# Splitting the second layer's weights and rows ahead of time, and a bank's products in one run

## The chip, the cores and the metric

One NeuronCore of a Trainium2 chip runs the whole program. The metric is the device time of one execution in microseconds (us). TensorE does the matrix products, VectorE (DVE) and ScalarE (ACT) read its results out of PSUM and prepare its operands, GpSimd (POOL) helps on SBUF data alone, and nearly all transfers between DRAM and SBUF are issued in order by SyncE's queue (SP).

## The reference

A row block x of 2048 tokens by 1024 goes through one retention layer and one layer of windowed attention. Cut to what matters:

```python
# layer 1, retention: 4 heads, chunks of 128 rows, a running state S per head
proj = rmsnorm(x, a_norm_g) @ a_w_in          # q, k, v (4x512), gate (4x512)
o = rms(retention(q, k, v)) * silu(gate)
x = x + o @ a_w_out
# layer 2, attention over the row's own and the previous block of 128 rows
k, v = split(rmsnorm(x, kv_norm_g) @ w_kv);  k = rmsnorm(k, k_norm_g)     # 2 kv heads of 64
q, gate = split(rmsnorm(x, b_norm_g) @ b_w_in);  q = rmsnorm(q, b_q_norm_g)  # 16 heads of 64
p = softmax(q @ k.T / 8 + bias, masked, with a sink per head)
x = x + ((p @ v) * silu(gate)) @ b_w_out
# rms(x) = x * rsqrt(mean(x * x) + 1e-6)
```

## The kernel before

Every product of float32 operands is made of three float32r products of a high and a low part: `hi*hi`, `hi*lo`, `lo*hi`. The high part is a ScalarE copy to float32r, the low part is what the subtraction leaves. All four banks of a projection (`pbank`, tags a and b with two buffers each) are taken by every projection, so the next one can write bank 0 only when bank 0 of the one before has been read out.

The rows are taken in 4 groups of 512 (`T`). **Phase a** is the retention: 16 units, one for each group and head. A unit is `main` (the projections `project_qk` and then `plain_vg` or, from unit 4 on, `strassen`), `ret` (the recurrence over 4 chunks) and `out_a` (two halves of `out_proj`, which adds into the residual rows `x1`). `drive` interleaves the `main` of one unit with the `ret` of the unit before. Small staging work (`stage_sums`, `row_stats`, `stage_rows`) is a generator in the list `behind`, one step of which is emitted at each `step()`, 18 of them in a unit with `strassen`. When a group's last head is out, its rows go to DRAM (`xmid`) and their sums of squares to `sqs`.

**Phase b** is the attention: 8 units, one for each group and key/value head. `work` yields the projections in order (`keys` once a group, `queries`, `gates`, `out_b`, and `out_last` for the last unit), and `plan` says how many of these steps go into each of 66 slots, between which one chunk of attention (`scores`, `scale`, `turn`, `values`, `gated`) is emitted. The agenda (`at`) adds small work some steps later. The steps and the plan fix the program order; a scheduler of the framework orders each engine's queue from it.

What the change touches in phase b: `wload` loads a piece of weights of 128 x 1024 and splits it (ACT copy on L127, subtraction on POOL on L132, or on DVE on L134 when the weights are first scaled by the norm's gain on L124 and kept in DRAM). `prep` does this for group 0's rows at the end of phase a, after multiplying them by the row norm (L195); `rows` does it for groups 1 to 3 with POOL's multiplication on L964, ACT's copy on L968 and DVE's subtraction on L969. Those rows' tiles have one buffer, so a group's rows go in when the gates of the group before have been computed.

Of the kernel before, what the change touches and what calls it, by code (L numbers as in the profile page):

```python
# [12 lines left out]
F32 = mybir.dt.float32  # L13
# [6 lines left out]
P = 128  # L20
D = 1024
# [15 lines left out]
PIECE = 512  # L37
# [21 lines left out]
def tile_yoco(ctx, tc, x, x_t, w_qk, w_vg, wo_a, w_kv, w_b, wo_b, ag, kvg, bg, kng, qng,  # L59
# [15 lines left out]


# [34 lines left out]
    scaled = {}  # L111

    def wload(src, cols, name, kscale=None, key=None):

        kn = 1024 // cols
        if key in scaled:
            src, kscale = scaled[key], None
# [4 lines left out]
        if kscale is not None:  # L122
            for k in range(kn):
                nc.vector.tensor_scalar_mul(raw[:, k, :], raw[:, k, :], kscale[:, k : k + 1])  # L124
            scaled[key] = dram.tile([P, kn, cols], F32, name=f"ws_{name}")
            nc.sync.dma_start(scaled[key], raw)
        nc.scalar.copy(hi, raw)  # L127
        if psum["phase"] == "b" and kscale is None:

            for k in range(0, kn, PIECE // cols):  # L130
                t = (slice(None), slice(k, k + PIECE // cols))
# [5 lines left out]
    def proj(src, nk, xhi, xlo, feat, evac, name, kscale=None, key=None, cols=512, before=None):  # L137
        kn = 1024 // cols
        bk = [pbank("ab"[m // 2], f"pp_{name}_{m}") for m in range(4)]
        for kp in range(nk // kn):  # L140
            if before is not None:
                before(kp)
            hi, lo = wload(src[kp], cols, f"{name}_{kp}",
                           None if kscale is None else kscale[:, kp * kn : (kp + 1) * kn],
                           (key, kp))
            for kk in range(kn):
                k = kp * kn + kk
                st, sp = k == 0, k == nk - 1
                kx = xhi[0].shape[1]
                xh, xl = xhi[k // kx][:, k % kx, :], xlo[k // kx][:, k % kx, :]  # L150
                for m in range(4):
                    sl = slice(m * P, (m + 1) * P)
                    o = bk[m][:, :cols]
# [8 lines left out]
            yield  # L162
        for m in range(4):
            evac(m, bk[m])
# [6 lines left out]
    def stats(g, tiles, tag):  # L171
# [6 lines left out]
        ss = small.tile([P, MT], F32, tag="ssx", bufs=2, name=f"ssb_{g}")  # L178
        nc.vector.tensor_copy(ss, ps[:, :MT])
        r = rsqrt_mean(ss, D, MT, f"b_{g}")  # L180
# [4 lines left out]
        rb = small.tile([P, T], F32, tag="rb", bufs=1, name=f"rb_{g}")  # L185
        nc.vector.tensor_copy(rb, rp)
        return rb

    def prep(g, rb):

        xhi, xlo = xt_tiles(f"b{g}")
        for kp in range(KT // 2):
            raw = wp.tile([P, 2, T], F32, tag="raw", bufs=RAW, name=f"xraw_b{g}_{kp}")
            nc.sync.dma_start(raw, xmid[g][kp])
            nc.vector.tensor_tensor(raw, raw, rb.unsqueeze(1).to_broadcast([P, 2, T]), op=ALU.mult)  # L195
            hi, lo = xhi[kp], xlo[kp]
            nc.scalar.copy(hi, raw)
            nc.vector.tensor_tensor(lo, raw, hi.bitcast(F32), op=ALU.subtract)
            yield
        return xhi, xlo  # L200

    def out_proj(src, ohi, olo, evac, name):
        for half in range(2):
            yield from proj(src[half], 4, ohi, olo, True,
                            lambda m, ps, half=half: evac(half * 4 + m, ps), f"{name}_{half}")
# [22 lines left out]
    first = {}  # L228


    def phase_a(pa):
# [110 lines left out]

        def strassen(n, src, xt, evac, after):
# [13 lines left out]
            for p in range(7):  # L357
# [3 lines left out]
                for i, w in enumerate(src(p)):  # L361
                    hi, lo = wload(w, 512, f"{n}_{p}{i}")
                    for kk in range(2):
                        k = i * 2 + kk
                        if p in (0, 1, 6):
                            k0 = k + KT // 2 * (p > 0)
                            xh, xl = (t[k0 // 2][:, k0 % 2, H * (p == 6) :] for t in xt)
                        else:
                            xh, xl = (t[:, k, :] for t in st["sum", SX[p - 2]])
                        start, stop = k == 0 and p in (0, 1, 3), k == KT // 2 - 1  # L370
                        for f in range(2):
                            sl = slice(f * P, (f + 1) * P)
# [301 lines left out]
        def prep_b0():  # L674
            rb = stats(0, [short(f"st_{i}") for i in range(2)], "rr")
            first["xt"] = yield from prep(0, rb)

        def out_a(u):
            g, h = units[u]
            ohi, olo, x1 = st.pop(("o", u))  # L680
            acc = []

            def evac(f, ps):
# [9 lines left out]
                if f == 0:  # L693
                    acc.append(stp(f"acc_{g}"))
                    nc.gpsimd.tensor_copy(acc[0], sq)
                else:
                    nc.gpsimd.tensor_tensor(acc[0], acc[0], sq, op=ALU.add)
                if f == KT - 1:
                    nc.sync.dma_start(sqs[g], acc[0])
# [14 lines left out]
        bias = bias_rows()  # L714
        for u in range(nu - 1):
# [521 lines left out]
```

## Time and profile before

| What | Value |
|---|---|
| Median of 3 runs (lowest to highest) | 2511.96 us (2510.32 to 2513.04) |
| The profiled execution: its own time, its span | 2509.29 us, 2507.5 us |
| TensorE products busy, mean granted clock | 97% of the span, 0.986 |
| VectorE, ScalarE, GpSimd busy | 67%, 45%, 20% |
| DMA queue 1 | 393 MB, 47.3% of 16 engines |

The span is the time from the first to the last instruction; the execution takes some 2 us more. A busy share says how much of a stretch an engine had an instruction in flight; the granted clock is the share of TensorE's 2.4 GHz that it was given, whose lower level is 1.2 GHz. Phase a takes the first 1652 us and phase b the rest.

### The profile page before, as it was taken

The numbers are of one execution on the slowest core, as the hardware profiler recorded it, in microseconds if no ns is written. First come the engines' busy times: TensorE is split into PE (matmuls) and PEld (weight loads), VectorE is DVE, ScalarE is ACT, GpSimd is POOL, SyncE is SP. The second block draws the span as 40 slices with busy tenths as digits, with TensorE's granted clock in tenths as the row PEclk, the third lists the DMA queues.
The fourth block names the chain that finished last, engine by engine and source line by source line (L and its number), as shares of the span: only waits on it lengthen the run. The fifth ranks groups of instructions, "written<-read, shape, count | busy, mean of one in ns | idle before, by whom it ended". The sixth has DMA issues, their size and how long they took to land.

```text
span 2507.5 us, 31994 instructions
## 1 busy us (share of the span) xinstructions
PE 2435.8 (97%) x11576; PEld 1976.3 (79%) x11576; DVE 1670.0 (67%) x2856; ACT 1118.1 (45%) x2060; POOL 495.8 (20%) x487
## 2 busy tenths in 40 slices
PE   8999999999999999999999999989899999989998
PEld 6888777888887888888888888778687777768776
DVE  5546675776867657678666576666766766676675
ACT  4333233544435445445354354435544545445452
POOL 0000000020000020000011000032444645455350
PEclk9999999999999999999999999989899999999999
DMA  8434883586636454465354343365243242342422
GB/s 291 138 111 136 261 274 118 171 288 226 233 113 199 136 180 151 151 219 182 121 193 164 101 147 113 114 241 185 76 143 128 91 148 68 135 149 87 141 94 86
DMA packets 141178, 395.09 MB, mean 158 GB/s; under 512 B 16427, under 2 KB 29020, under 8 KB 141020
## 3 DMA queue, kind: packets, MB, share of 16 engines
q1 hardware_dynamic: 141020, 393.05, 47.3%
q8 instruction: 91, 1.49, 0.2%
q14 instruction: 67, 0.55, 0.1%
HBM read 321.66 MB, written 74.47 MB: 158 GB/s over the span
## 4 chain that ended last, share of the span: by engine, by line
PE 75%; DVE 7%; DMA 4%; issue 1%; ACT 1%; POOL 0%; SPq 0%; ACTq 0%; DVEq 0%; POOLq 0%
PE pp_ao L157 4%; PE pp_ao L155 4%; PE pp_ao L156 4%; PE o_t L1052 2%; PE s_t L1003 2%; PE pp_bo L784 2%; PE pp_bo L785 2%; PE pp_bo L783 2%; PE pT_t L1034 1%; PE ot_r L649 1%; PE o_r L621 1%; PE o_r L623 1%; PE o_r L622 1%; PE dl_r L613 1%; DVE P_t L1006 1%
## 5 line engine op out<-in xcount | busy, mean ns | idle before, releaser
L107 POOL TENSOR_SCALAR r_o_r<-sso_r,ep 128x1 f32<-128x1 f32 x48 | 27.7, 578 | 910.3 <-ACT jo_r L643 910.3
L155 PE MATMUL pp_ao<-ohi_r,whi_ao 128*128 128x512 f32 x512 | 199.3, 393 | 7.5 <-DVE x_r L685 2.6
L156 PE MATMUL pp_ao<-olo_r,whi_ao 128*128 128x512 f32 x512 | 200.9, 392 | 0.0
L157 PE MATMUL pp_ao<-ohi_r,wlo_ao 128*128 128x512 f32 x512 | 196.6, 393 | 0.1
L1006 DVE CUSTOM_DVE_ANT_0 P_t<-s_t,bias,nsnk 128x256 f32<-128x256 f32 (+1 forms) x256 | 112.6, 470 | 70.1 <-PE s_t L1003 49.9
L127 ACT CAST whi_ao<-raw_ao 128x1024 fp32r<-128x1024 f32 x64 | 67.2, 1050 | 152.8 <-issue 47.3
L1016 ACT ACTIVATE P_t<-P_t,nm_t 128x128 f32<-128x128 f32 x256 | 100.5, 395 | 77.0 <-DVE P_t L1013 66.6
L134 DVE TENSOR_TENSOR wlo_ao<-raw_ao,whi_ao 128x1024 fp32r<-128x1024 f32 x64 | 78.1, 1223 | 83.2 <-ACT whi_ao L127 83.2
L1003 PEld LDWEIGHTS s_t<-kst,qst_b 128*128 128x128 f32 x512 | 78.8, 194 | 56.2 <-DVE nm_t L1006 32.1
L709 ACT CAST Shi_r<-S 128x512 fp32r<-128x512 f32 x120 | 69.9, 617 | 117.4 <-PE o_r L623 88.2
L1003 PE MATMUL s_t<-kst,qst_b 128*128 128x256 f32 (+1 forms) x512 | 96.5, 301 | 26.4 <-DVE nm_t L1006 26.1
L155 PEld LDWEIGHTS pp_ao<-ohi_r,whi_ao 128*128 128x128 f32 x512 | 96.7, 189 | 29.4 <-DVE x_r L685 3.4
L157 PEld LDWEIGHTS pp_ao<-ohi_r,wlo_ao 128*128 128x128 f32 x512 | 96.9, 190 | 21.8 <-DVE wlo_ao L134 1.4
L156 PEld LDWEIGHTS pp_ao<-olo_r,whi_ao 128*128 128x128 f32 x512 | 96.8, 189 | 20.2 <-issue 0.2
L710 DVE TENSOR_TENSOR Slo_r<-S,Shi_r 128x512 fp32r<-128x512 f32 x120 | 85.4, 737 | 40.0 <-ACT Shi_r L709 39.8
L636 DVE SCALAR_TENSOR_TENSOR S<-S,dl_r 128x512 f32<-128x512 f32 x112 | 74.7, 682 | 41.5 <-PE dl_r L615 41.3
L132 POOL TENSOR_TENSOR wlo_bo<-raw_bo,whi_bo 128x512 fp32r<-128x512 f32 x56 | 76.2, 1382 | 114.7 <-ACT whi_bo L127 75.8
L685 DVE TENSOR_TENSOR x_r<-x_r,pp_ao 128x512 f32<-128x512 f32 x128 | 83.8, 683 | 12.5 <-PE pp_ao L157 12.4
L784 PE MATMUL pp_bo<-olo_t,whi_bo 128*128 128x512 f32 x224 | 90.6, 404 | 0.0
L785 PE MATMUL pp_bo<-ohi_t,wlo_bo 128*128 128x512 f32 x224 | 89.1, 403 | 0.0
L783 PE MATMUL pp_bo<-ohi_t,whi_bo 128*128 128x512 f32 x224 | 85.5, 404 | 0.0
L107 POOL TENSOR_SCALAR r_o_r<-sso_r,es_a 128x1 f32<-128x1 f32 x16 | 8.1, 506 | 359.9 <-ACT jo_r L643 359.9
(1084 smaller groups left out, 7509.7 us busy)
## 6 DMA issues: line engine op xcount, KB each, us to landing
raw_ao<-in_wo_a SPq DMA_DIRECT2D x64, 512.0 KB, 3.6
b<-in_w_vg SPq DMA_DIRECT2D x64, 256.0 KB, 4.8
res<-xmid SPq DMA_DIRECT2D x56, 256.0 KB, 4.1
raw_bo<-in_wo_b SPq DMA_DIRECT2D x28, 512.0 KB, 3.5
x_r<-in_x_t SPq DMA_DIRECT2D x16, 512.0 KB, 6.0
xin<-in_x SPq DMA_DIRECT2D x16, 512.0 KB, 3.6
xmid<-x_r SPq DMA_DIRECT2D x16, 512.0 KB, 4.2
xraw_b<-xmid SPq DMA_DIRECT2D x16, 512.0 KB, 3.7
```

The lines of the kernel that those rows point to most:

```text
L134: nc.vector.tensor_tensor(lo, raw, hi.bitcast(F32), op=ALU.subtract)
L155: nc.tensor.matmul(o, hi[:, kk, sl], xh, start=st, stop=False)
L156: nc.tensor.matmul(o, hi[:, kk, sl], xl, start=False, stop=False)
L157: nc.tensor.matmul(o, lo[:, kk, sl], xh, start=False, stop=sp)
L685: nc.vector.tensor_tensor(t, t, ps, op=ALU.add)
L710: nc.vector.tensor_tensor(lo, src[:, d, :], hi.bitcast(F32), op=ALU.subtract)
L783: nc.tensor.matmul(o, hi[:, kk, sl], xh, start=s, stop=False)
L784: nc.tensor.matmul(o, hi[:, kk, sl], xl, start=False, stop=False)
L785: nc.tensor.matmul(o, lo[:, kk, sl], xh, start=False, stop=e)
L1003: nc.tensor.matmul(o, q[:, h, :], kst[:, kv * 2 + hl, kb + b0 : kb + 2, :], start=hl == 0, stop=hl == 1)
L1006: nc.vector.tensor_tensor_reduce(out=pt[:, j, :w], in0=o, in1=bias[:, kv * GQ + h, b0 * P :], scale=-1.0, scalar=nsnk[:, kv * GQ + h : kv ...
L1016: nc.scalar.activation(pt[:, i, :P], pt[:, i, :P], AF.Exp, scale=-1.0, bias=nm[:, i : i + 1], accum_out=den[:, i : i + 1])
```

## The change

In phase b no weights and no rows are split any more, but for the last group's rows. `stage_b` does it in phase a: in units 7, 8, 9, 11, 12 and 13 it loads nine pieces each of 128 x 512 of phase b's weights, multiplies them by the gain, makes the two parts on ACT and DVE and writes them to DRAM (`wb`). `out_a` splits the rows of groups 0 to 2 when they are complete (`split_row`, to `xb`). Phase b loads both parts straight into the operands' tiles. The rows are no longer multiplied by their norm: keys and queries are normalised anyway, with an epsilon that is scaled with the row (`eps`), values are multiplied by the row's factor as they leave PSUM, and gates by a row of factors (`rb`), one more DVE operation for each bank. In `proj`, `strassen` and `proj_b` (not in `project_qk`) the loop over banks goes outside that over a piece's blocks of 128, so that 6 (keys: 12) products go to one bank one after the other where it was 3. `out_proj` loads the first piece of its second half ahead of reading out the first. The plan gives the last unit but one fewer steps and the last one more.

```diff
-    def wload(src, cols, name, kscale=None, key=None):
+    def wload(src, cols, name):
...
-        if psum["phase"] == "b" and kscale is None:
-            for k in range(0, kn, PIECE // cols):
-                nc.gpsimd.tensor_tensor(lo[t], raw[t], hi[t].bitcast(F32), op=ALU.subtract)
-        else:
-            nc.vector.tensor_tensor(lo, raw, hi.bitcast(F32), op=ALU.subtract)
+        nc.vector.tensor_tensor(lo, raw, hi.bitcast(F32), op=ALU.subtract)
...
-            for kk in range(kn):
...
-                for m in range(4):
+            for m in range(4):
...
+                for kk in range(kn):
...
+        if then is not None:
+            then()
         for m in range(4):
             evac(m, bk[m])
...
+    def load_xb(g):
+        first["xt"] = xt = xt_tiles(f"b{g}")
+        for kp in range(KT // 2):
+            if g == NG - 1:
+                raw = wp.tile([P, 2, T], F32, tag="raw", bufs=RAW, name=f"xraw_{kp}")
+                nc.sync.dma_start(raw, xmid[g][kp])
+                yield
+                nc.scalar.copy(xt[0][kp], raw)
+                nc.vector.tensor_tensor(xt[1][kp], raw, xt[0][kp].bitcast(F32), op=ALU.subtract)
+                yield
+                continue
+            for i, t in enumerate(xt):
+                nc.sync.dma_start(t[kp].bitcast(F32), xb[g][kp][:, i])
+            yield
...
+        def stage_b(pieces):
+            nxt = None
+            for n, (src, dst, scale) in enumerate(pieces + [(None,) * 3]):
+                cur = nxt
+                if src is not None:
+                    t = p1.tile(list(src.shape), F32, tag="st", bufs=6, name=f"wraw_{n}")
+                    nc.sync.dma_start(t, src)
+                    nxt = t, dst, scale
+                if cur is not None:
+                    t, d, sc = cur
+                    hi, lo = (p1.tile(list(t.shape), F32R, tag="st", bufs=6, name=f"w{hl}_{n}") for hl in ("hi", "lo"))
+                    for k in range(t.shape[1]):
...
+                            nc.scalar.mul(hi[:, k, :], t[:, k, :], sc[:, k : k + 1])
+                            nc.vector.scalar_tensor_tensor(lo[:, k, :], t[:, k, :], sc[:, k : k + 1],
+                                                           hi[:, k, :].bitcast(F32), op0=ALU.mult, op1=ALU.subtract)
+                    for i, v in enumerate((hi, lo)):
+                        nc.sync.dma_start(d[:, i], v.bitcast(F32))
+                yield
...
+            def split_row(f):
+                t = x1[f // 2][:, f % 2, :]
+                hi, lo = (p1.tile([P, T], F32R, tag="st", bufs=6, name=f"xm{hl}_{g}_{f}") for hl in ("hi", "lo"))
+                nc.scalar.copy(hi, t)
+                nc.vector.tensor_tensor(lo, t, hi.bitcast(F32), op=ALU.subtract)
+                for i, v in enumerate((hi, lo)):
+                    nc.sync.dma_start(xb[g][f // 2][:, i, f % 2, :], v.bitcast(F32))
...
-                    acc.append(stp(f"acc_{g}"))
+                    acc.append(wp.tile([P, T], F32, tag="raw", bufs=RAW, name=f"acc_{g}"))
...
+            if u + 1 in (7, 8, 9, 11, 12, 13):
+                behind.append(stage_b(todo[:9]))
+                del todo[:9]
...
-        pre = prep_b0()
-        drive(tc, itertools.chain(out_a(nu - 2), itertools.islice(pre, 2)), ret(nu - 1), 1.5, 0)
-        for _ in itertools.chain(out_a(nu - 1), pre):
+        scales(0, [short(f"stb_{i}") for i in range(2)], "rr", small.tile([P, T], F32, tag="rb", bufs=1, name="rb_0"))
+        rows = load_xb(0)
+        drive(tc, itertools.chain(rows, out_a(nu - 2)), ret(nu - 1), 2, 0)
+        for _ in out_a(nu - 1):
             pass
...
+        def parts_of(key, kp, name):
+            d = wb[key][kp]
+            t = [wp.tile([P] + list(d.shape[2:]), F32R, tag=f"w{hl}", bufs=3, name=f"w{hl}_{name}_{kp}") for hl in ("hi", "lo")]
+            for i in range(2):
+                nc.sync.dma_start(t[i].bitcast(F32), d[:, i])
+            return t
...
-                nc.scalar.activation(t, ps, AF.Tanh, scale=0.5)
-                nc.vector.scalar_tensor_tensor(t, t, 1.0, ps, op0=ALU.add, op1=ALU.mult)
+                nc.vector.tensor_tensor(t, ps, scaled[g][2], op=ALU.mult)
+                th = p1.tile([P, T], F32, tag="th", bufs=2, name=f"th_{n}_{m}")
+                nc.scalar.activation(th, t, AF.Tanh, scale=0.5)
+                nc.vector.scalar_tensor_tensor(t, th, 1.0, t, op0=ALU.add, op1=ALU.mult)
...
-        for u in range(1, nu - 1):
+        for u in range(1, nu - 2):
             plan += [4, 4] + ([4, 4, 4] if units[u + 1][1] == 0 else [3, 3, 2]) + [3, 3, 2]
-        plan += [2, 2, 2, 1, 1, 3, 3, 2, 0]
+        plan += [3, 3, 3, 3, 3, 3, 3, 1] + [1, 2, 2, 2, 2, 1, 3, 3, 2]
```

## Rows read from the trace of the kernel before

**Rows 1.** The page: the span, TensorE's busy time, and the granted clock in 40 equal slices (9 is 0.9 or more).
```profile
span 2507.5 us, 31994 instructions
PE 2435.8 (97%) x11576; PEld 1976.3 (79%) x11576; DVE 1670.0 (67%) x2856; ACT 1118.1 (45%) x2060; POOL 495.8 (20%) x487
PEclk9999999999999999999999999989899999999999
```
**Rows 2.** Busy time by stretch (us from the span's start): the stretch's length, then busy us and count of PE, PEld, DVE, ACT and POOL, the granted clock, the DMA engines' busy share and GB/s.
```profile
280.00:390.00 110.00, 101.48 (x453) 81.94 (x452) 76.19 (x102) 35.81 (x48) 3.77 (x6) 0.98 0.77 254
390.00:700.00 310.00, 310.00 (x1424) 256.33 (x1423) 223.95 (x300) 139.55 (x200) 32.07 (x34) 1.00 0.62 208
...
1600.00:1680.00 80.00, 69.94 (x342) 58.59 (x341) 57.30 (x94) 28.60 (x52) 22.00 (x24) 0.91 0.47 158
1680.00:1800.00 120.00, 112.95 (x549) 88.04 (x547) 89.46 (x205) 63.36 (x145) 41.34 (x35) 0.97 0.50 174
1800.00:1990.00 190.00, 188.20 (x968) 147.80 (x968) 121.16 (x321) 93.19 (x248) 87.71 (x77) 0.98 0.33 110
1990.00:2020.00 30.00, 22.20 (x101) 16.33 (x100) 26.47 (x52) 16.99 (x45) 17.00 (x11) 0.83 0.38 123
2020.00:2200.00 180.00, 178.78 (x931) 141.21 (x930) 114.77 (x294) 86.15 (x219) 88.17 (x76) 1.00 0.34 114
2200.00:2230.00 30.00, 22.80 (x97) 16.43 (x96) 24.70 (x49) 16.11 (x44) 15.98 (x10) 0.83 0.38 123
...
2405.00:2508.00 103.00, 89.50 (x502) 68.78 (x500) 63.88 (x177) 39.49 (x121) 20.18 (x15) 0.95 0.29 98
```
**Rows 3.** What TensorE waited for from 1600 to 1670 us: who waited for whom, us in total, times, longest.
```profile
PE pp_b0k L787 <- ACT whi_b0k L127: 4.1, 1, 4.1
PE ot_r L649 <- DVE gate_a L646: 2.7, 1, 2.7
PE pp_b0k L787 <- DVE x_r L685: 0.7, 1, 0.7
```
**Rows 4.** The same from 1990 to 2030 us.
```profile
PE s_t L1003 <- DVE nm_t L1006: 7.4, 2, 4.0
```
**Rows 5.** VectorE from 1985 to 2020 us in order of time: start, us, instruction.
```profile
1998.59 1.78 DVE L874 TENSOR_TENSOR qs_b<-qn_b,qs_b 128x512 fp32r<-128x512 f32 x1
2000.29 2.29 DVE L969 TENSOR_TENSOR xlo_b<-xraw_b,xhi_b 128x1024 fp32r<-128x1024 f32 x1
...
2007.44 0.68 DVE L874 TENSOR_TENSOR qs_b<-qn_b,qs_b 128x512 fp32r<-128x512 f32 x1
...
2014.22 1.22 DVE L969 TENSOR_TENSOR xlo_b<-xraw_b,xhi_b 128x1024 fp32r<-128x1024 f32 x1
```
**Rows 6.** GpSimd in the same stretch.
```profile
1999.78 3.93 POOL L964 TENSOR_TENSOR xraw_b<-xraw_b,rb 128x512 f32<-128x512 f32 x2
2007.55 3.90 POOL L964 TENSOR_TENSOR xraw_b<-xraw_b,rb 128x512 f32<-128x512 f32 x2 [3.85 <-DMA xraw_b<-xmid]
```
**Rows 7.** TensorE in the middle of a projection: L155 to L157 are the three products of one block into one bank, and the next L155 goes to the next bank.
```profile
606.37 0.39 PE L156 MATMUL pp_ao<-olo_r,whi_ao 128*128 128x512 f32 x1
606.59 0.39 PE L157 MATMUL pp_ao<-ohi_r,wlo_ao 128*128 128x512 f32 x1
606.82 0.39 PE L155 MATMUL pp_ao<-ohi_r,whi_ao 128*128 128x512 f32 x1
```
**Rows 8.** Groups of instructions of the page: busy us and mean ns of one, idle before, and what ended it.
```profile
L127 ACT CAST whi_ao<-raw_ao 128x1024 fp32r<-128x1024 f32 x64 | 67.2, 1050 | 152.8 <-issue 47.3
L134 DVE TENSOR_TENSOR wlo_ao<-raw_ao,whi_ao 128x1024 fp32r<-128x1024 f32 x64 | 78.1, 1223 | 83.2 <-ACT whi_ao L127 83.2
L709 ACT CAST Shi_r<-S 128x512 fp32r<-128x512 f32 x120 | 69.9, 617 | 117.4 <-PE o_r L623 88.2
L710 DVE TENSOR_TENSOR Slo_r<-S,Shi_r 128x512 fp32r<-128x512 f32 x120 | 85.4, 737 | 40.0 <-ACT Shi_r L709 39.8
L132 POOL TENSOR_TENSOR wlo_bo<-raw_bo,whi_bo 128x512 fp32r<-128x512 f32 x56 | 76.2, 1382 | 114.7 <-ACT whi_bo L127 75.8
L685 DVE TENSOR_TENSOR x_r<-x_r,pp_ao 128x512 f32<-128x512 f32 x128 | 83.8, 683 | 12.5 <-PE pp_ao L157 12.4
```
**Rows 9.** DMA issues of the page: tensor, count, size, median us from issue to landing.
```profile
b<-in_w_vg SPq DMA_DIRECT2D x64, 256.0 KB, 4.8
...
raw_bo<-in_wo_b SPq DMA_DIRECT2D x28, 512.0 KB, 3.5
```
**Rows 10.** Busy time by stretch as in rows 2, in units 10 and 11 (unit 11 begins at 1117 us).
```profile
1070.00:1090.00 20.00, 20.00 (x102) 16.88 (x101) 18.93 (x29) 12.96 (x20) 1.58 (x2) 1.00 1.00 339
...
1110.00:1130.00 20.00, 20.00 (x91) 16.46 (x91) 8.53 (x11) 6.32 (x9) 1.34 (x2) 1.00 0.19 66
1130.00:1150.00 20.00, 20.00 (x93) 16.44 (x93) 12.20 (x19) 5.96 (x9) 0.82 (x2) 1.00 0.26 78
```
**Rows 11.** Waits of the whole span: VectorE for the staged weights of `stage_sums`.
```profile
DVE b L335 <- DMA b<-in_w_vg: 30.5, 11, 5.5
```
**Rows 12.** What TensorE waited for from 2400 to 2510 us.
```profile
PE pT_t L1034 <- DVE P_t L1028: 4.3, 1, 4.3
PE s_t L1003 <- DVE nm_t L1006: 3.7, 4, 1.1
```

More of the change, by code (lines that the diff above doesn't have):

```diff
@@ L74, in tile_yoco @@
     sqs = [dram.tile([P, T], F32, name=f"sqs{i}") for i in range(NG)]
+    parts = lambda shape, name: dram.tile([P, 2] + shape, F32, name=name)
+    xb = [[parts([2, T], f"xb{i}_{kp}") for kp in range(KT // 2)] for i in range(NG - 1)]
+    wb = {"k": [parts([4, 256], f"wk{kp}") for kp in range(2)]}
+    for kv in range(KVH):
+        wb["q", kv], wb["g", kv] = ([parts([2, T], f"w{n}{kv}_{kp}") for kp in range(4)] for n in "qg")
+        for half in range(2):
+            wb["o", kv, half] = [parts([2, T], f"wo{kv}{half}_{kp}") for kp in range(2)]
     neghalf = const.tile([P, GQ], F32, name="neghalf")
@@ L184, in stats, with ahead @@
         nc.tensor.matmul(rp, ones, dg, start=True, stop=True)
-        rb = small.tile([P, T], F32, tag="rb", bufs=1, name=f"rb_{g}")
         nc.vector.tensor_copy(rb, rp)
[L187 to L200, printed above, removed]
-    def out_proj(src, ohi, olo, evac, name):
-        for half in range(2):
-            yield from proj(src[half], 4, ohi, olo, True,
-                            lambda m, ps, half=half: evac(half * 4 + m, ps), f"{name}_{half}")
+        scaled[g] = r, eps, rb
+    def out_proj(src, ohi, olo, evac, name):
+        pre = []
+        def ahead():
+            pre.extend(wload(src[1][0], 512, f"{name}_1_0"))
+        yield from proj(src[0], 4, ohi, olo, True, evac, f"{name}_0", then=ahead)
+        yield from proj(src[1], 4, ohi, olo, True, lambda m, ps: evac(4 + m, ps), f"{name}_1", first=pre)
     bdr = dram.tile([QH, P, 384], F32, name="bdr")
@@ L362, in strassen @@
                     hi, lo = wload(w, 512, f"{n}_{p}{i}")
[L363 to L372, printed above, removed]
+                    for f in range(2):
+                        sl = slice(f * P, (f + 1) * P)
+                        for kk in range(2):
+                            k = i * 2 + kk
+                            if p in (0, 1, 6):
+                                k0 = k + KT // 2 * (p > 0)
+                                xh, xl = (t[k0 // 2][:, k0 % 2, H * (p == 6) :] for t in xt)
+                            else:
+                                xh, xl = (t[:, k, :] for t in st["sum", SX[p - 2]])
+                            start, stop = k == 0 and p in (0, 1, 3), k == KT // 2 - 1
                             kw = dict(skip_group_check=True)
@@ L697, in evac @@
                     nc.gpsimd.tensor_tensor(acc[0], acc[0], sq, op=ALU.add)
+                if f % 4 == 3 and g < NG - 1:
+                    for i in range(f - 3, f + 1):
+                        split_row(i)
                 if f == KT - 1:
-                    nc.sync.dma_start(sqs[g], acc[0])
+                    if g == NG - 1:
+                        first["acc"] = acc[0]
+                    else:
+                        nc.sync.dma_start(sqs[g], acc[0])
             yield from out_proj(wo_a[h], ohi, olo, evac, f"ao{u}")
@@ L759, in phase_b @@
         nchunk = nu * MT * 2
-        st = {"xt": first["xt"], "step": 0}
+        st = {"step": 0}
         agenda = {}
@@ L789, in proj_b @@
                             nc.tensor.matmul(o, xl[:, sl], hi[:, kk, :], start=False, stop=e)
-                    if not e and (kk + 1) * cols % 512 == 0:
+                    if m == 1 or m == 3 and kp < nk // kn - 1:
                         yield
@@ L800, in keys @@
             n = f"b{g}k"
-            yield from proj_b(w_kv, KT, st["xt"], False, n, kscale=kvgs, key="kv", cols=256)
+            yield from proj_b("k", KT, first["xt"], False, n, cols=256)
+            r_x, eps = scaled[g][:2]
             if g and not kb:
@@ L1102, in work @@
                 if u + 2 < nu and units[u][1] == 0:
-                    at(12, scales, units[u + 2][0])
-                yield from out_b(u - 1)
-                if u + 1 < nu:
+                    at(12, row_scales, units[u + 2][0])
+                if u < nu - 1:
+                    yield from out_b(u - 1)
                     if units[u + 1][1] == 0:
```

147 lines of the change are left out of this document (70 added, 77 removed).

## The prediction

> **What bounds the kernel now.** I read the page first: TensorE has products in flight for 2435.8 of 2507.5 us and the granted clock is full in all but two of 40 slices [rows 1]. So at most some 72 us of idle time and a little lost clock can be won unless the products themselves get shorter. They don't: their number is unchanged, and in the middle of a projection one starts every 0.22 or 0.23 us, both within a bank (L156 to L157) and where the next bank begins (L157 to L155) [rows 7]. I take 0.227 us.
>
> Next came the busy time by stretch, to see where the missing time lies [rows 2]. The loss of a stretch is its idle time plus the clock that was not granted, (1 - granted) x length. From 390 to 700 us it is 0, with VectorE busy for 224 of 310 us; from 2020 to 2200 us it is 1.2. The loss is in clumps:
>
> - 1600 to 1680, where the retention ends: 10.1 + 0.09 x 80 = 17.3 us.
> - 1680 to 1800, first attention units: 7.1 + 3.6 = 10.7.
> - 1800 to 1990: 1.8 + 3.8 = 5.6.
> - 1990 to 2020, rows of group 2 coming in: 7.8 + 0.17 x 30 = 12.9.
> - 2200 to 2230, the same for group 3: 7.2 + 5.1 = 12.3.
> - 2405 to 2508, the tail: 13.5 + 5.2 = 18.7.
>
> Together 77.5 us, and outside phase b another 10.7 at 280 to 390 (8.5 + 2.2). Then the waits and the order of time in the clumps. At the first, keys' products wait 4.1 us for the ACT copy of the first weights, behind the rows' preparation [rows 3]. At the third, scores wait 7.4 us for VectorE in two waits [rows 4]; VectorE is subtracting row parts there, 2.29 us for one while GpSimd multiplies rows and 1.22 us for the same operation later, and 1.78 against 0.68 us for the same split of queries [rows 5, 6]. So what sets the end is TensorE's stream of products, stretched where VectorE's queue is long at the change of a group.
>
> **The change part by part, against the profiled execution of 2509.3 us** (2.7 us under the median of the runs).
>
> *Splitting leaves phase b.* A piece cost 1.05 us on ACT and two subtractions of 1.38 us on GpSimd [rows 8]; 26 pieces a group (2 keys, 8 each of queries, gates and output). GpSimd is left with small operations, so the rival for VectorE's operands in rows 5 and 6 goes. The rows' subtractions (1.2 to 2.3 us each) and GpSimd's multiplications ahead of them go for groups 1 and 2; for group 3 the ACT copy and the subtraction stay. What each clump gives back:
>
> - 1600 to 1680: the waits of 4.1 and 0.7 us go, since weights and rows come ready by DMA [rows 3], and so should the lost clock of 7.2, which follows that idle time; the retention's own wait of 2.7 us (ot_r) stays. That is 12.0; with nearly 1 us of the 2.5 idle us that no listed wait explains, I take 13.
> - 1680 to 1800: first scaling and splitting of weights on VectorE and group 1's rows go. I take 8 of 10.7.
> - 1800 to 1990: 2 of 5.6.
> - 1990 to 2020: of 12.9 I take 10. A quiet stretch still loses 1.2 in 180 us, and VectorE still has gates and queries at once.
> - 2200 to 2230: 8 of 12.3, as group 3's rows are still split.
> - Tail: waits of 4.3 and 3.7 us for VectorE [rows 12] can be filled with the products that the plan moves into the last slots, two steps of 12 products of half width where there were none, 2 x 12 x 0.113 = 2.7 us. With the splitting of the last weights gone from GpSimd I take 4 of 18.7.
>
> Sum 45. From both sides: 0 if other work takes every freed place, 77.5 if all the loss goes.
>
> *The gates' extra operation.* Four more VectorE operations on 512 columns a unit, 0.68 us each by the reading of a bank in rows 8 (L685): 2.7 us a unit, 22 us in all. VectorE was busy 115 of 180 us in a quiet stretch [rows 2], so this hides; beside the clumps it is inside what I left there.
>
> *More transfers in phase b.* A piece is now two loads of 512 KB, each on the queue with a median of 3.5 us to landing [rows 9]. A piece feeds 24 products, 24 x 0.227 = 5.4 us, and three pairs of tiles are in flight, so a load has some 11 us until it is needed. Changes of group are 210 us apart, 1990 to 2200; the extra bytes are 26 x 0.52 = 13.6 MB in that time, 65 GB/s on top of 114 [rows 2], and 339 GB/s has been moved without TensorE losing a product [rows 10]. Cost 0; if the cover goes, a late pair costs what the first rival below says. The queue is in order: behind a load that waits for its tile stand residual rows and stores, none due sooner than a piece.
>
> *Staging in phase a.* 52 pieces of 512 columns, each one ACT operation (0.62 us by L709), one on VectorE (0.74 by L710) [rows 8], one load and two stores; 24 rows likewise. That adds 47 us to ACT and 56 to VectorE over some 800 us, where VectorE had slack and TensorE none. The nearest rows are the stretches with `stage_sums`: 0 lost at 390 to 700, but 10.7 at 280 to 390 [rows 2]. There VectorE waits for a staging load, 30.5 us in all, up to 5.5 at a time [rows 11], with the reading of banks queued behind it. Here a load is issued one step ahead (12 products, 2.7 us, or more) and takes 4.8 [rows 9], so ACT can wait, with casts of weights queued behind it; three pairs of tiles cover 11 us of that. Steps fall in the first half of the units; in unit 11 the engines are quiet there, with VectorE at 8.5 and 12.2 of 20 us and the DMA engines at 0.19 and 0.26 [rows 10]. `split_row` takes eight tiles of six, so its fourth row waits for a store, once in each half of three units. Bounds 0 and nine units times 10.7 = 96; nearest the Strassen units of 390 to 700, so 3 us.
>
> *Order of the banks.* The pace in rows 7 says 0. Bank 0 is complete 18 products before the end of a projection and not 9, 4.1 against 2.0 us, for a reading of 0.68: more slack where VectorE is late, but those waits are in clumps already counted. The first weights of `out_proj`'s second half now stand ahead of its readings (1.05 + 1.22 us [rows 8]), inside the new slack. Bounds 0 and a gain of 2 to 4 at 280 to 390; I take 0.
>
> Sum: 2509.3 - 45 + 3 = 2467.3 in the profiled execution, 2470 in the median of runs.
>
> **The rivals.**
>
> *Weights land too late.* If the two loads of a piece land one after the other, 2 x 3.5 = 7.0 us against 5.4, the 18 pieces before and between the first attention chunks are each 1.6 us late: 28 us, so 2498. Later each of the 26 pieces of a group has 210 / 26 = 8.1 us, which covers it. For it: nothing but the products stands in that stretch. Against: 339 GB/s is far over one load in 3.5 us (150 GB/s), so loads overlap [rows 9, 10]. Chance 0.08. By the Trainium skill (SBUF — State Buffer, "The DMA setup-cost knee") a transfer has a fixed cost of about 2 us beside 436 GB/s; an estimate from that is 3.2 us for 512 KB, 6.4 for a pair in a row, 18 us late in all and 2488. The trace's 3.5 us for one agrees with it; what a pair takes no row shows.
>
> *The clumps stay.* If the burst is due to the number of operations at a change of group, gates' extra reads take the place of the rows' subtractions, the 18 us of groups 2 and 3 and half of the 8 at 1680 are not won: 45 - 22 = 23, so 2492. For it: VectorE is 26.5 of 30 us busy there [rows 2]. Against: much of that is operations at up to twice their length. Chance 0.12.
>
> *Staging stalls the retention* (the other side). If units 7, 8, 9, 11, 12 and 13 each lose what the stretch at 280 to 390 loses, 10.7 us, it costs 64 and leaves 2509.3 - 45 + 64 = 2528, 2531 in runs. It decides from 7.5 us a unit, 0.8 a piece. For it: the same shape of work, in-order engines, DMA already heavy near a group's end. Against: three staged units in a row lost nothing. Chance 0.10.
>
> *The change does nothing that can be measured*: clumps are refilled and staging costs the rest, say 2512 within 5 us. Chance 0.06.
>
> **How the numbers follow.** The forecast, 2470 with its own range of 2452 to 2486, has 0.64. It takes in staging from 0 to 15 us and clumps that give back up to 15 more. Range for 8 in 10: 2448 to 2502, which takes in the first two rivals. Runs of before lie within 0.1%, so 0.2% or 5 us is about what can be told from no change. Faster: 0.64 + 0.08 + 0.12 and a little of staging at half its price, 0.85. Same 0.06. Slower 0.09.
>
> **What would show it.** Right: no idle time over 2 us ahead of the first keys, and a granted clock near 1.00 there; the two stretches around a change of group without waits of scores for VectorE; row-sized splits of queries at 0.68 us throughout; GpSimd nearly empty in phase b; phase a's last product within 5 us of where it was. Wrong: TensorE waiting for DMA into weight tiles at the head of phase b (first rival), scores still waiting at group changes (second), or units 7 to 13 longer than the 103 us of phase a's mean with ACT or VectorE waiting for staging loads or for stores (third).

## The result and the profile after

The changed kernel takes 2492.38 us (median of runs from 2490.84 to 2498.07) against 2511.14: ratio 0.9931, interval [0.9912, 0.9949]. It is faster by 19 us where 42 were forecast (2470 against 2512); 2492 lies in the range of 2448 to 2502. Its profiled execution took 2491.95 us, 17.3 less than that of before.

The page answers [rows 1]: TensorE has as many products as before, GpSimd is half as busy, the granted clock is 0.9 or more in all slices.
```profile
span 2490.2 us, 32134 instructions
PE 2433.3 (98%) x11576; PEld 1966.7 (79%) x11576; DVE 1625.0 (65%) x2898; ACT 1052.9 (42%) x2024; POOL 234.1 (9%) x287
PEclk9999999999999999999999999999999999999999
```
TensorE's busy time fell by only 2.5 us, so nearly all that was won is idle time of TensorE. Where time was won and lost shows in the moments at which the first and last products of each part start. The table is made from the start times of the traces (us); each trace is of one execution, which can lie some us off the median of its kernel (e5_place: 2491.01 against 2487.11), so single differences of 2 or 3 us in it say little. "Units" are those of the retention, from one unit's first `qk` product to another's; "end" goes from the first `qk` product of unit 15 to the last output product, "second layer" from there to the last product of all. The runs named e1 to e13 come below.

| | start to unit 4 | units 4 to 7 | 8 to 11 | 12 to 14 | end | second layer |
|---|---|---|---|---|---|---|
| before | 410.1 | 412.6 | 402.3 | 290.6 | 136.0 | 851.9 |
| after | 405.7 | 418.3 | 413.9 | 294.1 | 144.8 | 809.6 |
| e8_order | 405.1 | 410.4 | 402.7 | 291.2 | 140.9 | 839.6 |
| e7_shift | 411.7 | 413.4 | 405.3 | 294.0 | 139.1 | 852.6 |
| e4_pool | 407.9 | 421.0 | 412.0 | 294.0 | 143.6 | 835.8 |
| e1_order | 412.0 | 426.7 | 418.8 | 297.2 | 146.7 | 825.1 |
| e3_little | 406.5 | 414.6 | 406.7 | 294.5 | 145.4 | 813.2 |
| e13_little_old | 413.8 | 415.3 | 411.4 | 296.9 | 145.0 | 824.0 |
| e5_place | 407.7 | 421.9 | 414.6 | 290.7 | 141.1 | 809.4 |
| e6_scales | 408.4 | 420.5 | 414.3 | 294.0 | 141.2 | 811.5 |
| e12_even | 406.0 | 410.8 | 401.9 | 294.8 | 141.2 | 812.0 |

The second layer won 42.3 us. The retention won 4.4 up to unit 4 and lost 29.6 behind it: its last output product, which the prediction wanted within 5 us of 1651.7, starts at 1676.8. So the question is what cost the retention 25 us.

A stretch can be compared only with the same work in the other kernel, and the second layer starts 25.1 us later after the change. So the stretches after are counted from events: from the start of the retention's last output product (1651.7 before, 1676.8 after) and, for the two changes of group, from the last product of the gates of units 3 and 5 (1999.2 and 2207.9 before, 2005.6 and 2204.5 after); the tail begins some 10 us ahead of the last gates' last product (2415.5 and 2404.3). Busy time by stretch, after (columns as in [rows 2]):
```profile
390.00:700.00 310.00, 310.00 (x1409) 253.54 (x1408) 230.98 (x312) 145.78 (x214) 29.82 (x34) 1.00 0.67 224
710.00:824.00 114.00, 109.68 (x498) 88.09 (x497) 87.07 (x112) 60.47 (x88) 10.40 (x12) 1.00 0.72 238
1123.00:1238.00 115.00, 110.15 (x496) 87.73 (x496) 86.64 (x113) 60.93 (x90) 10.62 (x12) 1.00 0.73 239
1625.00:1677.00 52.00, 46.05 (x193) 36.91 (x192) 22.36 (x35) 14.41 (x29) 8.98 (x11) 0.90 0.27 92
1677.00:1705.00 28.00, 26.77 (x169) 24.08 (x168) 7.50 (x30) 5.39 (x16) 8.34 (x12) 1.00 0.91 329
1705.00:1825.00 120.00, 115.20 (x570) 90.43 (x569) 66.25 (x193) 52.25 (x152) 18.34 (x17) 0.96 0.48 165
1825.00:1996.00 171.00, 169.81 (x892) 135.26 (x891) 101.20 (x294) 60.17 (x190) 22.53 (x26) 1.00 0.61 205
1996.00:2026.00 30.00, 28.67 (x149) 22.36 (x148) 21.53 (x62) 13.82 (x42) 0.00 (x0) 1.00 0.61 219
2197.00:2227.00 30.00, 28.38 (x152) 22.58 (x151) 22.14 (x59) 14.43 (x43) 0.00 (x0) 1.00 0.43 143
2394.00:2490.20 96.20, 85.25 (x486) 65.01 (x484) 58.22 (x169) 29.88 (x103) 0.00 (x0) 0.98 0.39 134
```
The first clump of the prediction, 1600 to 1680, is divided where the retention ends; in the kernel before:
```profile
1600.00:1652.00 52.00, 49.26 (x229) 39.82 (x227) 38.17 (x56) 19.89 (x36) 14.46 (x16) 1.00 0.31 102
1652.00:1680.00 28.00, 20.67 (x114) 18.78 (x114) 19.13 (x40) 8.71 (x17) 7.54 (x9) 0.76 0.75 263
```
Losses, reckoned as the prediction does (idle time plus the clock that was not granted), in us:

| Stretch | before | after | won | forecast |
|---|---|---|---|---|
| last 52 us of the retention | 2.7 | 11.1 | -8.4 | 0 |
| keys and first queries | 14.1 | 1.2 | 12.9 | 13 |
| first attention units | 10.7 | 9.6 | 1.1 | 8 |
| from there to the first change of group | 5.6 | 1.2 | 4.4 | 2 |
| first change of group | 12.9 | 1.3 | 11.6 | 10 |
| second change of group | 12.3 | 1.6 | 10.7 | 8 |
| tail | 18.7 | 12.9 | 5.8 | 4 |

The clump of the first attention units is still there, 25 us later:
```profile
1800.00:1820.00 20.00, 15.20 (x75) 11.17 (x75) 14.26 (x53) 13.29 (x48) 0.00 (x0) 0.74 0.18 60
```
Units 7 and 11 of the retention (the second and third row of the first list) now lose 4.3 and 4.9 us of TensorE with the DMA engines 0.72 and 0.73 busy. From 390 to 700 TensorE is never idle, yet it started 1409 products where before had 1424.

### The profile page after: what moved, and what is told of

Read it like the earlier page. It is cut to its first block, busy times and chain, and to the rows that moved or that the text cites. A ratio compares the mean times of both kernels' runs of the same rounds, so it can differ in the third digit from the quotient of the medians.

```text
span 2490.2 us, 32134 instructions
## 1 busy us (share of the span) xinstructions
PE 2433.3 (98%) x11576; PEld 1966.7 (79%) x11576; DVE 1625.0 (65%) x2898; ACT 1052.9 (42%) x2024; POOL 234.1 (9%) x287
## 4 chain that ended last, share of the span: by engine, by line
PE 71%; DMA 8%; DVE 6%; ACT 1%; issue 1%; SPq 1%; POOL 0%; ACTq 0%; DVEq 0%; POOLq 0%
PE pp_ao L146 4%; PE pp_ao L148 4%; PE pp_ao L147 4%; PE o_t L1100 2%; PE s_t L1051 2%; PE pp_bo L846 2%; PE pp_bo L847 2%; PE pp_bo L845 2%; DMA wraw<-in_w_b 1%; PE pT_t L1082 1%; PE ot_r L689 1%; PE o_r L661 1%; PE o_r L662 1%; PE o_r L663 1%; PE dl_r L653 1%
## 5 line engine op out<-in xcount | busy, mean ns | idle before, releaser
L114 POOL TENSOR_SCALAR r_o_r<-sso_r,ep 128x1 f32<-128x1 f32 x48 | 37.6, 783 | 920.0 <-ACT jo_r L683 920.0
L1085 ACT COPY pTs_t<-pT_t 128x512 f32<-128x512 f32 x64 | 37.3, 583 | 130.3 <-PE pT_t L1082 130.0
L686 DVE SCALAR_TENSOR_TENSOR gate_a<-o_r,r_o_r,gate_a 128x512 f32<-128x512 f32 x64 | 47.9, 748 | 36.3 <-POOL r_o_r L115 35.3
```

## The experiments

### Where the second layer's 42 us come from

**GpSimd's subtractions put back.**
```diff
  # parts_of, behind the two loads of a piece; the result is not used
+ nc.gpsimd.tensor_tensor(junk, v[0], v[1], op=ALU.subtract)   # per half of the piece
```


> The changed kernel with GpSimd's two subtractions of 128 x 512 for each of phase b's pieces put back, their result used by nobody. Theory: phase b won its 42 us mainly because GpSimd no longer reads SBUF beside VectorE; then 25 to 35 us are lost again, 2517 to 2527, and VectorE's split of queries is again up to 1.8 us. Rival (it was the work taken off ACT, VectorE and the chain of rows and weights): 2492 to 2497.

Measured 2517.6 us, ratio 1.0033 [1.002, 1.0046]; the second layer takes 835.8 us, 26.2 more than after. One group of VectorE, the split of the queries, in before, after and this run (mean ns of one after the bar):
```profile
L874 DVE TENSOR_TENSOR qs_b<-qn_b,qs_b 128x512 fp32r<-128x512 f32 x32 | 27.3, 852 | 3.2 <-ACT qs_b L873 2.8
```
```profile
L938 DVE TENSOR_TENSOR qs_b<-qn_b,qs_b 128x512 fp32r<-128x512 f32 x32 | 22.0, 687 | 8.6 <-ACT qs_b L937 8.1
```
```profile
L943 DVE TENSOR_TENSOR qs_b<-qn_b,qs_b 128x512 fp32r<-128x512 f32 x32 | 27.3, 852 | 5.9 <-ACT qs_b L942 5.6
```
852 ns with GpSimd working beside it, 687 without, 852 again with operations whose result nobody reads. GpSimd is busy for 361.0 us of the second layer before, 95.7 after and 366.6 in this run, and the same 1387 operations of VectorE take 480 us after and 564 here. TensorE waits for the loads of weights only 0.7 us in this run, so it is not that the added reads hold the weights' tiles longer. So 26 of the 42 us are VectorE no longer slowed by GpSimd. The Trainium skill states the mechanism (SBUF — State Buffer, "Who interferes with whom": a VectorE instruction with two SBUF inputs contends with a GpSimd instruction that reads SBUF); the run agrees.

**The order of the bank loops, alone and taken out.**
```diff
- for kk in range(kn):        # e8_order: this edit alone, in the kernel before
-     for m in range(4):      # e1_order: undone, all else as after
+ for m in range(4):
+     for kk in range(kn):
```


> Kernel before with the order of the bank loops of the change and nothing else (in all three projections). If the order is worth by itself what it was worth beside the rest (1.56% between the changed kernel and the run without it), the time falls to 2470-2480; if the order only pays where GpSimd is out of the way and the weights come ready, 2500-2510.

Measured 2495.68 us, 0.9946 [0.9928, 0.9965]: neither of the two times expected. The order alone is worth 14 us in the trace, 12.3 of them in the second layer. TensorE's waits there, before and with the order:
```profile
PE s_t L1003 <- DVE nm_t L1006: 26.1, 14, 4.0
```
```profile
PE s_t L1003 <- DVE nm_t L1006: 16.6, 12, 3.0
```
e4_pool has 15.6 and after 8.4 (ten waits, none over 1.2), so each edit shortens this wait of scores for VectorE. 12.3 and 26.2 make 38.5 of 42.3; they were measured beside different kernels.

> The changed kernel with the three loops over banks put back as they were (3 products to a bank, then the next bank); all else as changed. Theory: the retention lost 29 us for three separate reasons, and the order of the banks is one: products that read the row sums start every 233 ns and those of the output projection every 229 ns where it was 227, which over 168 products of a Strassen projection and 96 of an output projection is 0.9 us a unit, some 12 us in all. Then about 2480 us, and the two paces back at 227. Rival (staging alone makes the 29 us): no change, 2492.

Measured 2532.41 us, 1.0087 [1.0072, 1.0102]: the theory fell. The paces are those of the changed kernel, and without the order the rest of the change is slower than before; beside the rest, the order is worth 40 us, 24.6 in the retention and 15.5 behind it. The wait of scores is 10.0 us in this run, so most of the 15.5 lies elsewhere.

### What cost the retention 25 us: the addresses of tiles

In the middle of a Strassen product of unit 9, after (start and us): a product of the row sums (`xhi_S`, `xlo_S`) every 0.233 us, where [rows 7] have 0.22 and 0.23.
```profile
970.21 0.39 PE L414 MATMUL pp_a9vb<-whi_a9v,xhi_S 128*128 128x512 f32 x1
970.44 0.39 PE L415 MATMUL pp_a9vb<-wlo_a9v,xhi_S 128*128 128x512 f32 x1
970.67 0.40 PE L416 MATMUL pp_a9vb<-whi_a9v,xlo_S 128*128 128x512 f32 x1
970.91 0.40 PE L415 MATMUL pp_a9vb<-wlo_a9v,xhi_S 128*128 128x512 f32 x1
```
On average over the trace they start every 0.233 us, output products every 0.229, and plain `v`, gate, query and key products every 0.227 to 0.228, as before. e1 has the same paces, so the order isn't it. The change gives the pool of small tiles three new ones and takes one away, and all tiles of the pools behind it move by 64 bytes in each partition.
```diff
- junk = small.tile([P, DV + 64], BF16, ...)[:, :DV]
+ junk = small.tile([P, DV + 32], BF16, ...)[:, :DV]    # e5_place, in the kernel after
+ junk = small.tile([P, DV + 96], BF16, ...)[:, :DV]    # e7_shift, in the kernel before
```


> Changed kernel with one scrap tile (junk) 64 bytes per partition shorter, so that all tiles behind the pool of small tiles lie again at the addresses they had in the kernel before (the output tiles of the retention at byte 126464 of a partition, a multiple of 128, in place of 126528). Placement theory (the new scale tiles pushed these tiles by 64 bytes, and products that read them went from 0.2267 us to 0.229 to 0.233): the paces go back to 0.2265-0.2275 us in the output products, the Strassen products that read the sums and the output products of phase b, and 10 to 13 us are won, 0.983-0.985 of the changed kernel's 2492 in tenths of a per cent 0.5: some 2480. Rival (the slower pace comes from more transfers or from the order): paces stay 0.229-0.233 and the time 2492.

> Kernel before with the scrap tile 64 bytes per partition longer and nothing else. Placement theory: the same products go from 0.2267 to 0.229-0.233 us and the kernel loses 8 to 13 us, 1.003-1.005. Rival: paces as before, 1.000.

e7_shift: 2521.2 us, 1.0044 [1.0027, 1.0061], 11 us slower for 64 bytes of unused padding, 12 in the trace's retention. Every engine has the same instructions in the same order as in the kernel before, and so have e5_place and after. The same place in it, and in e5_place:
```profile
968.35 0.39 PE L376 MATMUL pp_a9va<-whi_a9v,xlo_S 128*128 128x512 f32 x1
968.58 0.39 PE L375 MATMUL pp_a9va<-wlo_a9v,xhi_S 128*128 128x512 f32 x1
968.82 0.39 PE L376 MATMUL pp_a9va<-whi_a9v,xlo_S 128*128 128x512 f32 x1
```
```profile
974.89 0.39 PE L416 MATMUL pp_a9vb<-whi_a9v,xlo_S 128*128 128x512 f32 x1
975.12 0.39 PE L415 MATMUL pp_a9vb<-wlo_a9v,xhi_S 128*128 128x512 f32 x1
975.35 0.39 PE L416 MATMUL pp_a9vb<-whi_a9v,xlo_S 128*128 128x512 f32 x1
975.57 0.39 PE L414 MATMUL pp_a9vb<-whi_a9v,xhi_S 128*128 128x512 f32 x1
```
0.233 and 0.227 to 0.228 us on average over the traces: the placement theory holds. But e5_place took 2487.11 us, 0.9912 [0.9896, 0.9929], 5 below after and not 12: units 12 to 14 and the end are 7 us shorter, while units 4 to 7 got 3.6 longer. Unit 7 alone got 6.7 us longer (113.3 to 120.0), amid the staged pieces of the next section; why the same program waits longer there with its addresses put back is not shown.

### What cost the retention 25 us: the staged pieces

**Nearly no staging.** Six pieces instead of 52; the second layer reads one shared tile, so its weights are left out.
```diff
- wb["q", kv], wb["g", kv] = ([parts([2, T], f"w{n}{kv}_{kp}") for kp in range(4)] for n in "qg")
+ wb["q", kv], wb["g", kv] = [one] * 4, [one] * 4       # the same for "o"; pieces_b gives 4 + 2 pieces
```


> The changed kernel with 6 staged pieces where there were 52: all weights of queries, gates and output are loaded from one staged tile, so that phase b moves the same bytes with wrong weights. Theory: staging costs what units 6 to 11 lost beyond the order's share, some 10 us, so 2482. Rival (staging alone makes the 29 us): 2465 or less. Prediction's size for it (3 us): 2489.

Measured 2483.19 us, 0.989 [0.9873, 0.9906]: 9 us less than after; in the trace 3.7 less in units 4 to 7 and 7.2 in units 8 to 11. That is the price of staging in the changed kernel. What waited for it in after (690 to 1320 us):
```profile
ACT whi L362 <- DMA wraw<-in_w_b: 38.3, 18, 4.1
DVE wlo L363 <- ACT whi L362: 12.2, 9, 2.5
```
TensorE's listed waits in that time come to 9 us, none over 1.5. The clearest single case is unit 7 of e5_place, ScalarE and then VectorE in order of time:
```profile
735.15 0.72 ACT L362 ACTIVATE whi<-wraw,bgs 128x512 fp32r<-128x512 f32 x1 [4.46 <-DMA wraw<-in_w_b]
738.67 0.72 ACT L362 ACTIVATE whi<-wraw,bgs 128x512 fp32r<-128x512 f32 x1 [2.80 <-DMA wraw<-in_w_b]
```
```profile
735.91 0.75 DVE L363 SCALAR_TENSOR_TENSOR wlo<-wraw,bgs,whi 128x512 fp32r<-128x512 f32 x1 [3.32 <-ACT whi L362]
736.58 0.68 DVE L676 SCALAR_TENSOR_TENSOR S<-S,dl_r 128x512 f32<-128x512 f32 x1
740.74 0.75 DVE L363 SCALAR_TENSOR_TENSOR wlo<-wraw,bgs,whi 128x512 fp32r<-128x512 f32 x1 [3.48 <-DMA wq<-wlo]
741.40 0.69 DVE L760 TENSOR_TENSOR Slo_r<-S,Shi_r 128x512 fp32r<-128x512 f32 x1
742.01 0.68 DVE L543 TENSOR_TENSOR q_a<-pp_a7qk,cos_a 128x512 f32<-128x512 f32 x1
742.61 0.68 DVE L544 TENSOR_TENSOR th_a<-pp_a7qk,sin_a 128x512 f32<-128x512 f32 x1
```
```profile
PE pp_a7va L414 <- DVE th_a L544: 7.4, 1, 7.4
```
ScalarE waits for the load of a piece, VectorE for ScalarE and then for a store to free a tile, the reading of the `qk` banks stands behind both, and TensorE (last row) waits 7.4 us for that. Nor did the pieces run where the code lists them: those of units 8 and 12 were scheduled ahead. So 18 of the 52 pieces (22 of 56 pairs of operations, as a piece of the keys' weights has two) ran from 692 to 764 us in e5_place, around the start of unit 7, and 18 more around that of unit 11. Against e8_order, which has the same addresses and order, units 7, 9 and 11 of e5_place lost 10.2, 3.7 and 8.6 us and unit 13, with 7 pieces, none. The loss differs between runs that list the same pieces: with the addresses of after, unit 7 takes 109.7 us without staging (e3_little), 113.3 in after, and 115.6 to 116.3 in e2, e4 and e6.

**The same pieces elsewhere.**
```diff
- if u + 1 in (7, 8, 9, 11, 12, 13):      # 9 pieces each (7 in the last)
+ {1: 4, 4: 4, 5: 2, 9: 8, 10: 3, 13: 10, 14: 13, 15: 8}   # e9_spread, on e5_place
+ nxt = t, dst, scale; yield              # e10_slow: a piece in two steps, units as in e5_place
+ {8: 8, 9: 8, 10: 4, 12: 8, 13: 8, 14: 8, 15: 8}          # e12_even, on e11_both
```


> e5_place with the 52 staged pieces spread otherwise over the units (4, 4, 2, 8, 3, 10, 13 and 8 pieces in units 1, 4, 5, 9, 10, 13, 14 and 15, none in 7, 8, 11 and 12). In e5_place the staged pieces ran in four clumps, 22 pieces in unit 7 and 18 in unit 11 among them (those listed for units 8 and 12 were scheduled ahead into 7 and 11), and these units lost 10 and 9 us against the run with the bank order alone, while unit 13 with 7 pieces lost nothing. Theory (the clumps stall ScalarE and VectorE on their own loads): 15 to 22 of e5_place's 24 us between units 4 and 12 come back, 2467-2472. Rival (each piece costs what its operations cost, wherever it stands): the loss moves to units 13 to 15, 2485.

> e5_place with the same pieces in the same units, but one piece in two steps instead of one a step, so that each piece's load has twice the time. If ScalarE's and VectorE's waits for the loads of the pieces make the loss, units 7, 9 and 11 lose under 8 us together in place of 22 and the time is 2472-2478; if the work of the pieces makes it, 2485-2490.

e9_spread 2498.41 us, 0.9957 [0.9944, 0.997]; e10_slow 2494.82, 0.9941 [0.9925, 0.9957]. Both times lie above all that was expected. In e9_spread units 7 to 11 lost nothing against e8_order, but unit 2 lost 8.6 us, units 3 to 6 together 9, unit 13 3.3, and unit 14, which got 11 operations of pieces every 20 us, 8.6, with the same wait:
```profile
PE pp_a14va L414 <- DVE th_a L544: 6.1, 1, 6.1
```
In e10_slow units 7, 9 and 11 lose 9.5 in place of 22.5, and units 10 and 13 lose 12.5 anew. Neither "each piece has its price" (unit 9 of e9_spread took 8 for nothing) nor "twice the time for a load" fits. The next run asks whether their density does.

> e11_both with the pieces listed evenly over the lighter units: 8 each in units 8, 9, 12, 13, 14 and 15 and 4 in unit 10 (those of 8 and 12 are scheduled ahead into 7 and 11). In e9_spread 16 operations of pieces in unit 9 cost nothing and 12 in unit 13 nothing, while 11 in every 20 us of unit 14 cost 8.6 us. If density decides, units 9, 10, 13, 14 and 15 lose nothing and 7 and 11 2 to 4 us each: 2476-2482. If every piece has its price, 2490-2495.

Measured 2471.09 us, 0.9845 [0.9832, 0.9859]: 39 us below the kernel before and, by the ratios, some 21 below the changed one. Its last output product starts 4.4 us behind that of e8_order, with all 52 pieces staged, and from 690 to 1320 us TensorE's listed waits are two for a cast:
```profile
PE pp_ao L146 <- ACT whi_ao L125: 3.0, 2, 2.0
```
So where the pieces run decides what they cost. That it is their density is not shown, and some rows speak against it. Around the starts of units 11 and 14 of e12_even 12 pieces run in 36 and 41 us, as close together as the 18 of e5_place in 62 to 67, and cost 0 and 1.2 us; they end 18 us into the unit, those of e5_place 44 to 49, behind the reading of the `qk` banks. Unit 13 of e12_even has 18 pieces at about the same spacing as the 11 pieces there in e10_slow (4 or 5 in 20 us) and loses 2.4 us where e10_slow loses 6.3. Unit 2 of e9_spread lost its 8.6 us with no piece in it. Whether a cluster's length or its place in the unit counts, no run separates.

### The end of the retention

```diff
- rows = load_xb(0)
- drive(tc, itertools.chain(rows, out_a(nu - 2)), ret(nu - 1), 2, 0)
+ for _ in load_xb(0): pass
+ drive(tc, out_a(nu - 2), ret(nu - 1), 1.5, 0)
```


> The changed kernel with the loads of group 0's rows emitted before the last interleaving and not inside it, and the interleaving's ratio back at 1.5. Theory: the four steps of loads have no products, so the last unit's first chunks of retention run without the output projection's products beside them, and the projection is left for the end, where two waits of 2.7 us for VectorE have nothing to cover them: about 11 us come back, 2481. Rival (staging alone): 2492.

Measured 2497.73 us, 0.9956 [0.994, 0.9973], and the stretch stays at 71 us: this theory fell. The waits there, after, are
```profile
PE ot_r L689 <- DVE gate_a L686: 5.5, 2, 2.8
PE pp_ao L146 <- ACT ohi_r L694: 0.5, 1, 0.5
```
The last two chunks of the retention run with no output product of unit 14 left between them. In e2 too, since in both kernels (after and e2_end) the products of the row scales, moved ahead of the last unit's retention, stand in TensorE's queue before it and 26 output products go by meanwhile.
```diff
- scales(0, ...); rows = load_xb(0)
- drive(tc, itertools.chain(rows, out_a(nu - 2)), ret(nu - 1), 2, 0)
+ rows = rows()      # scales, then load_xb(0)
+ drive(tc, itertools.chain(out_a(nu - 2), itertools.islice(rows, 2)), ret(nu - 1), 1.5, 0)
```


> Changed kernel with the row scales of group 0 and its row loads put back behind the output products of unit 14, where the kernel before has them, at its ratio of 1.5. Theory: emitted ahead of the last unit's retention, the products of the scales stand in TensorE's queue before that retention, 26 products of unit 14 run out while it waits, and its last two chunks run with nothing between them; put back, the stretch from the last Strassen product of unit 15 to the last output product goes from 72 to 61-63 us, the kernel to 2481-2485. Rival (the last chunks wait for something else, their chain through VectorE or the loads): the stretch stays at 71-73 us and the time at 2492.

> e9_spread with the row scales and loads of group 0 behind the output products of unit 14 as in e6_scales. There the end of the retention got 4 us shorter in the trace and the median did not move. If that was real, 2-4 us below e9_spread, 2465-2469; if the earlier retention only takes the time elsewhere, as e9_spread within 2 us.

e6_scales 2494.4 us, 0.9942 [0.9925, 0.9959]; e11_both 2495.92, 0.9943 [0.9931, 0.9955] against e9_spread's 0.9957. The stretch from the last Strassen product went from 72 to 65 us, but part of the retention now stands before it: the whole end is 141.2 in place of 144.8 in e6 and 141.0 in place of 144.1 in e11. So 3 to 4 us in the traces; in the median of e6 it doesn't show, in that of e11 2.5 us do, inside both intervals. Nor are the 3 to 4 us shown to be the scales': e5_place, where nothing of this is moved, has 141.1, with the same idle time of TensorE in the stretch as after (5.95 us of 141 and of 145) but a granted clock of 0.99 where after has 0.96. e8_order has 140.9 as well, 4.9 over before's 136.0, with the order alone. Why is not settled.

### What makes the order worth more beside the rest

> e3_little (6 staged pieces in place of 52, the second layer reads one shared tile, so the weights of the second layer are left out) with the order of the bank loops of the kernel before, as in e1_order. There the old order cost 40 us beside the rest of the change, 25 of them in the retention, while the new order by itself won the kernel before only 1 us in the retention and 12 behind it. If the order's worth in the retention is slack that hides the staging, the old order costs e3_little 0 to 8 us in the retention and 12 to 16 behind it, 2498-2508; if it is worth 25 us there with or without staging, 2520-2524.

Measured 2511.48 us, 1.0 [0.9989, 1.0011], between the two: the order is worth 28 us without the staging. In the table, e13 against e3: 7.3 us ahead of unit 4, 0.7 in units 4 to 7, 4.7, 2.4, -0.4, and 10.8 in the second layer. e1 against after: 6.3, 8.4, 4.9, 3.1, 1.9, 15.5. So the slack that hides staging is some 8 of the 40, in units 4 to 7; the second layer, where nothing is staged, has 4.7 more with staging as well, unexplained. What of the change makes the order worth more than its 14 in the other parts stays open.

## Why the prediction was right and wrong

In the traces the second layer won 42.3 us, near the forecast's 45, and the retention lost 25.1 where the sum had 3 for staging and nothing else. So the step that made the forecast fail is the account of the retention: it took the pace of the products as fixed and gave the new tiles no term, and it priced staging by a stretch in which hardly any of the pieces ran. That the second layer came out as forecast is in part luck, as the next two terms show.

**Splitting leaves phase b, 45 us: 42.3 measured, but only with the order's help.** GpSimd off VectorE's back is 26 of it, as argued from rows 5 and 6. Without the new order the second layer won 26.8 (851.9 to 825.1 in e1_order), so 45 was too much for this term. By place, the keys' stretch (12.9 won, 13 forecast), the changes of group and the tail went as forecast or better, and the wait of 4.1 us [rows 3] is gone. The first attention units did not: 8 of 10.7 us were to go with the scaling and splitting there, and 1.1 went. GpSimd does nothing in the worst 20 us of it, 1800 to 1820, so it isn't the cause; what is stays open. The last 52 us of the retention lost 11.1 us where the prediction left its one wait of 2.7.

**Order of the banks, 0: failed, in the kernel's favour.** The pace was rightly no reason, and "those waits are in clumps already counted" was wrong: the order is worth 14 us by itself and 40 beside the rest, 15.5 of them in the second layer. The edit priced at nothing filled up what the term before had too much.

**The pace of 0.227 us in any order: failed, some 12 us.** Not for the order, but for the new tiles' sizes: products that read moved tiles take 0.229 to 0.233, some 12 us in e7_shift. The three scale tiles had no term at all in the sum.

**Staging, 3 us: mis-sized, 9 in after and up to 22.** The step that failed took the quiet stretch 390 to 700 for its nearest row, on pieces spread over the first halves of six units. Twice 18 pieces ran together around the start of one unit, with the mechanism of the third rival where a trace shows it clearly (e5_place: ACT waiting for a load, the reading of banks behind it, 7.4 us), at 2.1, 2.9 and 7.1 us in units 7, 9 and 11 of after against before, the slower pace included, short of the 7.5 in each of six units from which that rival decides. e12_even comes near the 3 with the pieces listed elsewhere: its retention ends 4.4 us behind that of e8_order.

**A moved step without a term.** Row scales of group 0 went ahead of the last retention; the prediction listed what leaves that stretch, not what now stands in TensorE's queue before it. In after the last two chunks run with no output product between them; 3 to 4 us in two traces at most, and not shown to be due to it.

**Gates' extra operation and more transfers, 0: nothing speaks against.** VectorE is busy for 101.2 of 171 us between the first attention units and the change of group, where the quiet stretch of [rows 2] had 114.8 of 180; with up to 329 GB/s moved at the head of the second layer, the weights' loads cost TensorE single waits of 1.2 and 0.9 us. The first rival did not come.

The retention's 25 us are, by these runs, about -1.4 (order) + 12 (addresses) + 9 (staging) = 20, with up to 3.6 for the scales. These were measured one at a time, and e5_place shows that they don't simply add. Undone together they do account for it: e12_even, with the old addresses, the pieces elsewhere and the scales moved back, ends its retention at 1654.7 us, 3.0 behind before. Its 2471.09 us are the forecast time, with a gain by the order in them that the forecast did not have.

## What to carry to other kernels

Before pricing an edit, ask what its new tiles push: a changed pool size moves every tile behind it, and one run with only padding changed tells what that is worth. Background work whose engines wait for its loads, with other work queued behind it, is priced by where it really runs, not by its sum: read its start times from the trace, since a scheduler can run two helpings together. The same edit can be worth 14 us alone and 40 beside others; price it in the kernel into which it goes. And compare stretches of two traces by what runs in them, not by their times.

## What the runs showed of the hardware

- 64 bytes more of padding per partition slowed products whose operands lie behind it from 0.227 to 0.233 us (Strassen sums) and 0.229 us (output products), 11 us of a kernel (e7_shift, with the same instructions in the same order); putting the addresses back restored the pace (e5_place). Which operand, and at which multiples, was not tried.
- GpSimd operations whose result nobody reads lengthened a VectorE split of 128x512 from 687 to 852 ns on average, and the kernel by 25 us (e4_pool).
